# 64 first products of a dense expert mixer made ahead of its loop, in buffers shared with later tiles, instead of 40

## The chip, the core and the metric

The kernel runs on one core of a Trainium2 chip. The metric is the device time of one execution in microseconds; lower is better. The core has five engines with a queue each: TensorE (PE) multiplies matrices, VectorE (DVE) and ScalarE (ACT) work on rows, GpSimd (POOL) issues the indirect DMAs here, and SyncE (SP) issues most other DMAs. Matrix products land in PSUM, everything else lies in SBUF.

## The reference, cut to what matters

The model block has a token mixer (latent attention and an RWKV-7 scan) and then an expert mixer over 512 tokens, 1024 wide. The change concerns the second alone:

```python
def peer_ffn(h, w_query, sub_keys1, sub_keys2, expert_down, expert_up):
    q = (h @ w_query).reshape(B, S, PEER_HEADS, 2, HALF_KEY)
    ...  # top 16 of 128 keys for each half, then top 16 of the sums: expert_idx, gates
    u = jnp.take(expert_down, idx_blk, axis=0)
    act = jax.nn.gelu(jnp.einsum('bpd,bphkd->bphk', h_blk, u))
    vv = jnp.take(expert_up, idx_blk, axis=0)
    return jnp.einsum('bphk,bphkd->bpd', g_blk * act, vv)
```

Each token uses 128 of the 16384 experts (8 heads x 16).

## The kernel before, in words

**Two ways for the experts.** The tokens stand in four blocks of 128. Blocks 0 and 1 gather their experts: for each of 128 slots POOL issues an indirect DMA (line 1152) of one row per token, down and up side by side (1 MB in all), VectorE multiplies and sums (line 1156), ScalarE applies gelu and the gate, and VectorE adds the scaled row to the accumulator (line 1163). Blocks 2 and 3 (`DENSE`, `nd` = 256 tokens) instead go through all 16384 experts, as 128 groups i of 128: a first product (experts of the group x tokens, over 1024 channels, 8 steps) gives the activations, gelu follows, the gates multiply, which are zero for experts that a token hasn't chosen, and a second product adds the result times the up rows to four PSUM banks.

**The first product** is made by `dense_z(i)` (line 1202). For i < AZ + PZ = 40 it is made ahead, in plain fp32: 8 steps of one fp32 product, each of which the trace records as two matmuls, with the raw tile `u_raw` and the tokens' rows `hf`. For i from 40 on it is made in the loop: `hi_lo` (line 1186) splits `u_raw` into `uh` (a cast on ScalarE) and `ul` (a subtraction on VectorE), and the tokens' rows are split once in `dense_h` into two tiles `hh` and `hl`; three products `uh hh`, `uh hl`, `ul hh` per step make 24 matmuls. The activations of the first AF_ = 24 lie in the tile `Af`, the next 8 in a tile `A`, the last PZ = 8 go to DRAM (`zd`) and come back into `Af` in the loop.

**The stages.** (1) After the scan, `tails` computes the last blocks' query products, the top keys and the chosen indices; at each of its steps two products ahead are put in at a lower priority (ZLATE), up to ZFIRST = 24. (2) `dense_spread` (line 1241) makes the dense gates from indices and weights: for each token VectorE builds one-hot rows, TensorE multiplies them into a bank `ps_G`, and from there VectorE multiplies the first AF_ groups straight into `Af` (line 1290), while ScalarE copies the others to a buffer `g_` that is stored to the DRAM table `gd` (line 1291) once for every TB = 16 tokens. At each such step one product ahead is made. (3) The loop of `dense` (line 1294 on) runs over i: it loads `v_raw`, splits it, multiplies activations by the gates `G` (line 1334) where these were not met in PSUM, splits the result into `ch` and `cl`, and lets TensorE add the twelve 512-column matmuls of the group before. G comes from `gd` for 8 groups at a time (line 1307). The buffers of `g_` and `G` are one ring of NG = 3.

**The order of the work.** A scheduler orders each engine's instructions by priority and by its own model of their times; on the chip the order of an engine is fixed. The gathers are put in with a lower priority (LATE), two slots for each iteration of the loop, and fill what is left; they have four buffers `gl`, and POOL's next gather waits until VectorE has used one up. The order of SP's DMAs is fixed too: a load that waits for its buffer holds up those behind it. `u_raw` and `v_raw` have four buffers each.

Of the kernel before, what the change touches and what calls it, by code (L numbers as in the profile page):

```python
# [19 lines left out]
P = 128  # L20
# [13 lines left out]
PRE = 2  # L34
LATE = 1000
ZLATE = 100
ZFIRST = 24
AZ = 32
AF_ = 24
PZ = 8  # L40
NG = 3
BG = [[0.91, 2, 2, 1.0, 2.2, 2.85, 2.45, 1.0], [1.6, 2.28, 1, 0.58, 0.25, 0.5, 0.13, 0.36]]
ZSTEP = 2
ADA = 1
# [112 lines left out]
def _build(ctx, tc, nc, A, out):  # L157
# [1015 lines left out]

    TB = 16
    HB = 8
    SUB = 8
    GSC = 2.0 ** 14
    nd = len(DENSE) * P  # L1180
    dn, ahead = {}, {}
    zd = dp.tile([P, PZ, nd], F32, name="zd")
    NJ = P // SUB - AF_ // SUB
    gd = dp.tile([P, NJ, nd // TB, SUB * TB], F32, name="gd")

# [3 lines left out]

    def dense_open():  # L1190
        dn["z"] = dz = pool("dz")
        dn["h"] = [dz.tile([P, KT, nd], F32R, name=f"h{c}") for c in "hl"]
        dn["act"] = {}
        dn["first"] = dz.tile([P, AF_, nd], F32, name="Af")
        dn["hf"] = dz.tile([P, KT, nd], F32, name="hf")

    def dense_h(b, h2T):
        q = DENSE.index(b)
        S.copy(dn["hf"][:, :, q * P:(q + 1) * P], h2T)
        hi_lo(*(t[:, :, q * P:(q + 1) * P] for t in dn["h"]), h2T)  # L1200

    def dense_z(i):

        dz = dn["z"]
        hh_, hl_ = dn["h"]
        if i < AF_:
            act = dn["first"][:, i]
        elif i < AZ:
            if i % SUB == 0:
                dn["A"] = dz.tile([P, SUB, nd], F32, name="A", tag="A", bufs=(AZ - AF_) // SUB)  # L1210
            act = dn["A"][:, i % SUB]
        elif i < AZ + PZ:
            act = dz.tile([P, nd], F32, name="zp", tag="zp", bufs=2)
        else:
            act = dn["v"].tile([P, nd], F32, name="act", tag="act", bufs=2)
        u = dz.tile([P, D], F32, name="u_raw", tag="u", bufs=4)
        nc.sync.dma_start(u, A["dense"][i, 0])
        if i < AZ + PZ:
            zs = ((u, dn["hf"]),)
        else:  # L1220
            uh = dz.tile([P, D], F32R, name="uh", tag="uh", bufs=2)
            ul = dz.tile([P, D], F32R, name="ul", tag="ul", bufs=2)
            hi_lo(uh, ul, u)
            zs = ((uh, hh_), (uh, hl_), (ul, hh_))
        ps = bank("ps_z", "pr", 3)
        for k in range(KT):
            ks = slice(k * P, (k + 1) * P)
            for m, (l, h) in enumerate(zs):
                mm(ps[:, :nd], l[:, ks], h[:, k], k + m == 0, k == KT - 1 and m == len(zs) - 1)
        S.activation(act, ps[:, :nd], AF.Gelu_apprx_tanh)  # L1230
        if AZ <= i < AZ + PZ:
            nc.scalar.dma_start(zd[:, i - AZ], act)
        else:
            dn["act"][i] = act

    def dense_ahead():
        for i in range(AZ + PZ):
            dense_z(i)
            yield

# [53 lines left out]
    def dense(sel):  # L1294

        n = nd
        for _ in dense_spread(sel):
            step(ahead["z"])
        drain(ahead["z"])
        dn["v"] = de = pool("de", side="right")  # L1300
        parts = {}

        def gates_of(j):

            if j < P // SUB:
                parts[j] = dn["g"].tile([P, n // TB, SUB, TB], F32, name="G", tag="G", bufs=NG)
                nc.sync.dma_start(parts[j].rearrange("p s c t -> p s (c t)"), gd[:, j - AF_ // SUB])

        for j in range(NG - 1):
            gates_of(AF_ // SUB + j)  # L1310
        acc = [[bank(f"acc{q}{d}", *(("px", 2) if q == 0 else (("pm", 1), ("po", 1))[d])) for d in range(2)]
               for q in range(len(DENSE))]
        prev = None
        for i in range(P + 1):
            if i < P:
                if i % SUB == 0:
                    if i >= AF_:
                        gates_of(i // SUB + NG - 1)
                    if AZ <= i + SUB < AZ + PZ:
                        t = dn["first"][:, i + SUB - AZ:i + 2 * SUB - AZ]  # L1320
                        nc.sync.dma_start(t, zd[:, i + SUB - AZ:i + 2 * SUB - AZ])
                        for j in range(SUB):
                            dn["act"][i + SUB + j] = t[:, j]
                if i >= AZ + PZ:
                    dense_z(i)
                act = dn["act"].pop(i)
                v = dn["w"].tile([P, D], F32, name="v_raw", tag="v", bufs=4)
                nc.sync.dma_start(v, A["dense"][i, 1])
                vh = de.tile([P, D], F32R, name="vh", tag="vh", bufs=2)
                vl = de.tile([P, D], F32R, name="vl", tag="vl", bufs=2)  # L1330
                hi_lo(vh, vl, v)
                a3 = act.rearrange("p (s t) -> p s t", t=TB)
                if i >= AF_:
                    V.scalar_tensor_tensor(a3, a3, 1.0 / GSC, parts[i // SUB][:, :, i % SUB], op0=ALU.mult, op1=ALU.mult)
                ch = de.tile([P, n], F32R, name="ch", tag="ch", bufs=2)
                cl = de.tile([P, n], F32R, name="cl", tag="cl", bufs=2)
                hi_lo(ch, cl, act)
                cur = (ch, cl, vh, vl)
            if prev is not None:
                ch, cl, vh, vl = prev  # L1340
                for q in range(len(DENSE)):
                    qs = slice(q * P, (q + 1) * P)
                    for d in range(2):
                        ds = slice(d * 512, (d + 1) * 512)
                        for m, (a, b) in enumerate(((ch, vh), (ch, vl), (cl, vh))):
                            mm(acc[q][d], a[:, qs], b[:, ds], i == 1 and m == 0, i == P and m == 2)
            prev = cur
            yield
        gt2 = dn["z"].tile([P, D], F32, name="gt2", tag="u", bufs=4)
        nc.sync.dma_start(gt2, mrow[3:4, :].to_broadcast([P, D]))  # L1350
        for q, b in enumerate(DENSE):
            x2 = dn["w"].tile([P, D], F32, name="x2e", tag="v", bufs=4)
            y = dn["w"].tile([P, D], F32, name="y", tag="v", bufs=4)
            nc.sync.dma_start(x2, x2d[b * P:(b + 1) * P, :])
            for d in range(2):
                ds = slice(d * 512, (d + 1) * 512)
                V.tensor_tensor(y[:, ds], acc[q][d], gt2[:, ds], op=ALU.mult)
                V.tensor_tensor(y[:, ds], y[:, ds], x2[:, ds], op=ALU.add)
            nc.sync.dma_start(out[b * P:(b + 1) * P, :], y)
        yield  # L1360
# [79 lines left out]
    def drain(gen):  # L1440
        for _ in gen:
            pass
# [28 lines left out]
    drain(streams[0])  # L1471
    nz = 0
    for _ in streams[1]:
        if "z" in ahead and nz < ZFIRST:
            tc.cur_priority += ZLATE
            step(ahead["z"], ZSTEP)
            tc.cur_priority -= ZLATE
# [28 lines left out]
```

## Time and profile before

| what | us |
|---|---|
| three runs, median (lowest to highest) | 1910.42 (1905.02 to 1913.4) |
| the profiled execution | 1907.93 |
| its span, first to last instruction | 1906.2 |
| TensorE busy | 1720.0 (90%) |
| VectorE busy | 1587.9 (83%) |
| ScalarE busy | 699.8 (37%) |
| GpSimd busy | 437.2 (23%) |

Busy time is counted from the start of an instruction to its end, where instructions that overlap count once. Matmuls are pipelined, so a busy TensorE is not TensorE at its peak. The stages matter more than the shares of the whole: the token mixer takes the first half and is not touched, and the products ahead, the spread and the loop stand in the second. Times in the rows are from the start of the span.

### The profile page before, as it was taken

The numbers are of one execution on the slowest core, as the hardware profiler recorded it, in microseconds if no ns is written. First come the engines' busy times: TensorE is split into PE (matmuls) and PEld (weight loads), VectorE is DVE, ScalarE is ACT, GpSimd is POOL, SyncE is SP. The second block draws the span as 40 slices with busy tenths as digits, with TensorE's granted clock in tenths as the row PEclk, the third lists the DMA queues.
The fourth block names the chain that finished last, engine by engine and source line by source line (L and its number), as shares of the span: only waits on it lengthen the run. The fifth ranks groups of instructions, "written<-read, shape, count | busy, mean of one in ns | idle before, by whom it ended". The sixth has DMA issues, their size and how long they took to land.

```text
span 1906.2 us, 30258 instructions
## 1 busy us (share of the span) xinstructions
PE 1720.0 (90%) x11018; PEld 1472.0 (77%) x11018; DVE 1587.9 (83%) x3654; ACT 699.8 (37%) x1727; POOL 437.2 (23%) x394
## 2 busy tenths in 40 slices
PE   5879999999899999999699979779999999999992
PEld 4667877778787698988388868657899988889892
DVE  4864446559778798888689999979999999999998
ACT  1233233321323232331131133335555555555551
POOL 1210010000222210222222222022333333333333
PEclk9889999999999999999899989879999999999996
DMA  9545654166986875889899889989999999999997
GB/s 385 196 154 172 230 174 161 44 217 204 365 333 211 345 247 190 298 312 362 330 351 351 317 302 316 293 330 399 400 403 416 415 416 415 414 408 415 411 373 281
DMA packets 146274, 588.75 MB, mean 309 GB/s; under 512 B 13886, under 2 KB 41918, under 8 KB 111564
## 3 DMA queue, kind: packets, MB, share of 16 engines
q1 hardware_dynamic: 76544, 284.69, 40.4%
q0 software_dynamic: 39360, 280.51, 38.2%
q10 hardware_dynamic: 30220, 21.60, 3.6%
q8 instruction: 87, 1.43, 0.3%
q14 instruction: 63, 0.52, 0.1%
HBM read 566.81 MB, written 19.94 MB: 308 GB/s over the span
## 4 chain that ended last, share of the span: by engine, by line
issue 31%; PE 31%; DVE 13%; POOL 12%; DMA 11%; ACT 1%; POOLq 0%; SPq 0%; ACTq 0%; DVEq 0%
POOL gl L1152 12%; DMA gl<-in_experts,ii 5%; PE ps_b L237 4%; PE ps_gt L237 4%; DMA w_b<-in_w_b 3%; PE ps_q L237 3%; DVE acc L1163 3%; PE ps_z L237 2%; DVE gl L1156 2%; PE ps_ap L237 2%; PE ps_y L237 1%; PE ps_m L237 1%; PE ps_G L237 1%; PE ps_M L237 1%; PE ps_s L237 1%
## 5 line engine op out<-in xcount | busy, mean ns | idle before, releaser
L1152 POOL DMA_INDIRECT gl<-in_experts,ii x256 | 382.9, 1496 | 989.1 <-DVE acc L1163 697.0
L1156 DVE SCALAR_TENSOR_TENSOR gl<-gl,h2p 128x1024 f32<-128x1024 f32 x256 | 311.3, 1216 | 49.8 <-DMA gl<-in_experts,ii 49.5
L1163 DVE SCALAR_TENSOR_TENSOR acc<-gl,z,acc 128x1024 f32<-128x1024 f32 x256 | 326.6, 1276 | 12.6 <-ACT z L1158 7.1
L237 PE MATMUL acc<-vl,ch 128*128 128x512 f32 x512 | 204.9, 400 | 7.4 <-DVE vl L1188 7.2
L237 PE MATMUL acc<-vh,cl 128*128 128x512 f32 x512 | 204.5, 399 | 5.0 <-DVE cl L1188 4.9
L237 PE MATMUL ps_z<-hh,uh 128*128 128x256 f32 x704 | 199.4, 283 | 0.0
L237 PE MATMUL ps_z<-hh,ul 128*128 128x256 f32 x704 | 199.4, 283 | 0.0
L237 PE MATMUL acc<-vh,ch 128*128 128x512 f32 x512 | 196.9, 397 | 2.7 <-ACT ch L1187 2.7
L237 PE MATMUL ps_z<-hl,uh 128*128 128x256 f32 x704 | 199.2, 283 | 0.0
L1157 ACT ACTIVATE z<-z 128x1 f32<-128x1 f32 x256 | 51.8, 203 | 368.0 <-DVE gl L1156 367.2
L237 PE MATMUL ps_z<-hf,u_raw 128*128 128x256 f32 x640 | 156.0, 388 | 8.4 <-ACT i1T L1264 8.4
L1188 DVE TENSOR_TENSOR vl<-v_raw,vh 128x1024 fp32r<-128x1024 f32 x128 | 156.0, 1219 | 4.6 <-ACT vh L1187 4.4
L237 PE MATMUL ps_gt<-hT,w_b 128*128 128x128 f32 x1024 | 136.9, 288 | 14.5 <-DMA w_b<-in_w_b 14.4
L237 PEld LDWEIGHTS ps_gt<-hT,w_b 128*128 128x128 f32 x1024 | 127.6, 201 | 20.9 <-DMA w_b<-in_w_b 11.5
L237 PEld LDWEIGHTS ps_z<-hl,uh 128*128 128x128 f32 x704 | 135.1, 192 | 3.8
L1187 ACT CAST vh<-v_raw 128x1024 fp32r<-128x1024 f32 x128 | 134.1, 1047 | 9.6 <-PE acc L237 4.8
L237 PEld LDWEIGHTS ps_z<-hh,uh 128*128 128x128 f32 x704 | 134.7, 191 | 3.4
L237 PEld LDWEIGHTS ps_z<-hh,ul 128*128 128x128 f32 x704 | 134.8, 191 | 0.3 <-DVE ul L1188 0.2
L237 PEld LDWEIGHTS ps_z<-hf,u_raw 128*128 128x128 f32 x640 | 117.1, 194 | 21.8 <-ACT i1T L1264 8.6
L237 PE MATMUL ps_b<-hT,w_b 128*128 128x128 f32 x896 | 123.6, 288 | 7.7 <-DMA w_b<-in_w_b 6.4
L237 PE MATMUL ps_q<-h2T,w_q 128*128 128x128 f32 x1024 | 125.6, 277 | 2.1 <-DMA w_q<-in_w_query 1.4
L237 PEld LDWEIGHTS ps_b<-hT,w_b 128*128 128x128 f32 x896 | 113.3, 200 | 18.0 <-DMA w_b<-in_w_b 6.3
(445 smaller groups left out, 3299.3 us busy)
## 6 DMA issues: line engine op xcount, KB each, us to landing
u_raw<-in_dense SPq DMA_DIRECT2D x128, 512.0 KB, 7.4
v_raw<-in_dense SPq DMA_DIRECT2D x128, 512.0 KB, 8.7
w_b<-in_w_b SPq DMA_DIRECT2D x82, 512.0 KB, 4.8
w_ada<-in_w_ada SPq DMA_DIRECT2D x48, 512.0 KB, 5.4
w_q<-in_w_query SPq DMA_DIRECT2D x48, 512.0 KB, 3.7
G<-gd SPq DMA_DIRECT2D x13, 1024.0 KB, 10.6
w_o<-in_w_o SPq DMA_DIRECT2D x24, 512.0 KB, 5.1
w_out<-in_w_out SPq DMA_DIRECT2D x24, 512.0 KB, 7.0
```

The costliest lines, as they stand in the source:

```text
L237: PE.matmul(o, l, r, start=start, stop=stop)
L1152: G.indirect_dma_start(out=gl, out_offset=None, in_=A["experts"], in_offset=bass.IndirectOffsetOnAxis(ap=ii[:, s:s + 1], axis=0))
L1156: V.scalar_tensor_tensor(gl[:, :D], gl[:, :D], 1.0, h2, op0=ALU.mult, op1=ALU.mult, accum_out=z[:, 0:1])
L1157: S.activation(z[:, 1:2], z[:, 0:1], AF.Gelu_apprx_tanh)
L1163: V.scalar_tensor_tensor(acc, gl[:, D:], z[:, 1:2], acc, op0=ALU.mult, op1=ALU.add)
L1187: S.copy(hi, x)
L1188: V.tensor_tensor(lo, x, hi.bitcast(F32), op=ALU.subtract)
```

## The change

AF_ rises from 24 to 32: the first 32 groups meet their gates in PSUM, and all 32 are put into the query stage, two at each step. 32 more (PZ), the groups 32 to 63, are made ahead, where it was 16: three at each of the spread's steps, of which there are now 8 since TB is 32, and the last 8 in the loop's first eight iterations, one each. Their activations lie in the buffers that later hold the split rows of the tokens (`hh`, `hl`, eight groups each) and the split weights (`uh`, `ul`, two buffers of four groups each). The split of the tokens' rows moves from `dense_h` into the loop's iteration 52 (`dense_split`), where those buffers are free again. So the loop makes split products for the groups 64 to 127 only. The tile `A` and the trip through `zd` are gone; the table `gd` has 12 instead of 13 parts of 8 groups, its rows are stored as 1024 instead of 512 bytes, and the ring of `g_` and `G` has two buffers instead of three.

```diff
--- before.py
+++ after.py
@@ -34,11 +34,9 @@
 PRE = 2
 LATE = 1000
 ZLATE = 100
-ZFIRST = 24
-AZ = 32
-AF_ = 24
-PZ = 8
-NG = 3
+AF_ = 32
+PZ = 32
+NG = 2
 BG = [[0.91, 2, 2, 1.0, 2.2, 2.85, 2.45, 1.0], [1.6, 2.28, 1, 0.58, 0.25, 0.5, 0.13, 0.36]]
 ZSTEP = 2
 ADA = 1
@@ -1173,13 +1171,12 @@
 
 
 
-    TB = 16
+    TB = 32
     HB = 8
     SUB = 8
     GSC = 2.0 ** 14
     nd = len(DENSE) * P
     dn, ahead = {}, {}
-    zd = dp.tile([P, PZ, nd], F32, name="zd")
     NJ = P // SUB - AF_ // SUB
     gd = dp.tile([P, NJ, nd // TB, SUB * TB], F32, name="gd")
 
@@ -1189,7 +1186,6 @@
 
     def dense_open():
         dn["z"] = dz = pool("dz")
-        dn["h"] = [dz.tile([P, KT, nd], F32R, name=f"h{c}") for c in "hl"]
         dn["act"] = {}
         dn["first"] = dz.tile([P, AF_, nd], F32, name="Af")
         dn["hf"] = dz.tile([P, KT, nd], F32, name="hf")
@@ -1197,30 +1193,34 @@
     def dense_h(b, h2T):
         q = DENSE.index(b)
         S.copy(dn["hf"][:, :, q * P:(q + 1) * P], h2T)
-        hi_lo(*(t[:, :, q * P:(q + 1) * P] for t in dn["h"]), h2T)
+
+    def dense_split():
+
+        dn["h"] = [dn["z"].tile([P, KT, nd], F32R, name=f"h{c}", tag=f"h{c}", bufs=1) for c in "hl"]
+        for k in range(0, KT, 2):
+            hi_lo(*(t[:, k:k + 2] for t in dn["h"]), dn["hf"][:, k:k + 2])
 
     def dense_z(i):
 
         dz = dn["z"]
-        hh_, hl_ = dn["h"]
         if i < AF_:
             act = dn["first"][:, i]
-        elif i < AZ:
-            if i % SUB == 0:
-                dn["A"] = dz.tile([P, SUB, nd], F32, name="A", tag="A", bufs=(AZ - AF_) // SUB)
-            act = dn["A"][:, i % SUB]
-        elif i < AZ + PZ:
-            act = dz.tile([P, nd], F32, name="zp", tag="zp", bufs=2)
+        elif i < AF_ + PZ:
+            tag, n, bufs = (("hh", 8, 1), ("hl", 8, 1), ("uh", 4, 2), ("ul", 4, 2))[(i - AF_) // 8]
+            if i % n == 0:
+                dn["zp"] = dz.tile([P, n, nd], F32, name="zp", tag=tag, bufs=bufs)
+            act = dn["zp"][:, i % n]
         else:
             act = dn["v"].tile([P, nd], F32, name="act", tag="act", bufs=2)
         u = dz.tile([P, D], F32, name="u_raw", tag="u", bufs=4)
         nc.sync.dma_start(u, A["dense"][i, 0])
-        if i < AZ + PZ:
+        if i < AF_ + PZ:
             zs = ((u, dn["hf"]),)
         else:
             uh = dz.tile([P, D], F32R, name="uh", tag="uh", bufs=2)
             ul = dz.tile([P, D], F32R, name="ul", tag="ul", bufs=2)
             hi_lo(uh, ul, u)
+            hh_, hl_ = dn["h"]
             zs = ((uh, hh_), (uh, hl_), (ul, hh_))
         ps = bank("ps_z", "pr", 3)
         for k in range(KT):
@@ -1228,13 +1228,10 @@
             for m, (l, h) in enumerate(zs):
                 mm(ps[:, :nd], l[:, ks], h[:, k], k + m == 0, k == KT - 1 and m == len(zs) - 1)
         S.activation(act, ps[:, :nd], AF.Gelu_apprx_tanh)
-        if AZ <= i < AZ + PZ:
-            nc.scalar.dma_start(zd[:, i - AZ], act)
-        else:
-            dn["act"][i] = act
+        dn["act"][i] = act
 
     def dense_ahead():
-        for i in range(AZ + PZ):
+        for i in range(AF_ + PZ):
             dense_z(i)
             yield
 
@@ -1295,8 +1292,7 @@
 
         n = nd
         for _ in dense_spread(sel):
-            step(ahead["z"])
-        drain(ahead["z"])
+            step(ahead["z"], 3)
         dn["v"] = de = pool("de", side="right")
         parts = {}
 
@@ -1316,13 +1312,12 @@
                 if i % SUB == 0:
                     if i >= AF_:
                         gates_of(i // SUB + NG - 1)
-                    if AZ <= i + SUB < AZ + PZ:
-                        t = dn["first"][:, i + SUB - AZ:i + 2 * SUB - AZ]
-                        nc.sync.dma_start(t, zd[:, i + SUB - AZ:i + 2 * SUB - AZ])
-                        for j in range(SUB):
-                            dn["act"][i + SUB + j] = t[:, j]
-                if i >= AZ + PZ:
+                if i >= AF_ + PZ:
                     dense_z(i)
+                else:
+                    step(ahead["z"])
+                if i == AF_ + PZ // 2 + 4:
+                    dense_split()
                 act = dn["act"].pop(i)
                 v = dn["w"].tile([P, D], F32, name="v_raw", tag="v", bufs=4)
                 nc.sync.dma_start(v, A["dense"][i, 1])
@@ -1471,7 +1466,7 @@
     drain(streams[0])
     nz = 0
     for _ in streams[1]:
-        if "z" in ahead and nz < ZFIRST:
+        if "z" in ahead and nz < AF_:
             tc.cur_priority += ZLATE
             step(ahead["z"], ZSTEP)
             tc.cur_priority -= ZLATE
```

## Rows read from the trace of the kernel before

**Rows 1.** Busy us of PE, PEld, DVE, ACT, POOL by stage; then PEclk, DMA share, GB/s

```profile
954.00:1126.00 172.00, 153.56 (x966) 139.58 (x966) 163.13 (x596) 41.06 (x121) 42.49 (x35) 0.97 0.90 333
1126.00:1248.00 122.00, 104.71 (x841) 88.84 (x840) 118.06 (x232) 45.60 (x106) 25.71 (x9) 0.91 0.93 300
1248.00:1390.00 142.00, 132.60 (x556) 104.66 (x557) 128.42 (x179) 72.81 (x139) 38.98 (x24) 0.94 0.99 387
1390.00:1868.00 478.00, 474.81 (x3010) 427.63 (x3009) 471.32 (x622) 262.35 (x524) 160.94 (x97) 1.00 1.01 406
1868.00:1906.20 38.20, 3.28 (x12) 2.10 (x12) 30.58 (x40) 4.88 (x19) 11.55 (x7) 0.60 0.76 282
```

**Rows 2.** The gathers' last instruction (line 1163) by stage: busy us, count, clock, DMA share, GB/s

```profile
954.00:1126.00 172.00, 42.03 (x34) 0.97 0.90 333
1126.00:1248.00 122.00, 12.74 (x10) 0.91 0.93 300
1248.00:1390.00 142.00, 28.10 (x22) 0.94 0.99 387
1390.00:1868.00 478.00, 122.41 (x96) 1.00 1.01 406
1868.00:1906.20 38.20, 12.81 (x10) 0.60 0.76 282
```

**Rows 3.** Costliest groups by shape from 1000 us on: busy us, mean ns, idle before

```profile
L1163 DVE SCALAR_TENSOR_TENSOR acc<-gl,z,acc 128x1024 f32<-128x1024 f32 x162 | 206.6, 1275 | 8.1 <-POOL acc L1147 5.0 <-ACT z L1158 3.0
L1156 DVE SCALAR_TENSOR_TENSOR gl<-gl,h2p 128x1024 f32<-128x1024 f32 x160 | 194.4, 1215 | 10.3 <-DMA gl<-in_experts,ii 10.1
L1188 DVE TENSOR_TENSOR ul<-u_raw,uh 128x1024 fp32r<-128x1024 f32 x88 | 107.6, 1223 | 0.2 <-ACT uh L1187 0.2
L1334 DVE SCALAR_TENSOR_TENSOR act<-act,G 128x256 f32<-128x256 f32 x88 | 36.5, 415 | 0.0
```

**Rows 4.** TensorE in order of time about the end of the query products

```profile
1094.77 16.57 PE L237 MATMUL ps_z<-hf,u_raw 128*128 128x256 f32 x76
...
1124.74 4.49 PE L237 MATMUL ps_z<-hf,u_raw 128*128 128x256 f32 x12 [8.39 <-ACT i1T L1264]
```

**Rows 5.** TensorE in order of time, in one iteration of the late loop

```profile
1385.28 0.28 PE L237 MATMUL ps_z<-hh,ul 128*128 128x256 f32 x1
1385.40 0.39 PE L237 MATMUL acc<-vh,ch 128*128 128x512 f32 x1
...
1388.15 0.28 PE L237 MATMUL ps_z<-hh,uh 128*128 128x256 f32 x1
```

**Rows 6.** Groups of VectorE instructions in the spread, 1126 to 1248 us

```profile
L1290 DVE SCALAR_TENSOR_TENSOR Af<-Af,ps_G 128x96 f32<-128x96 f32 x64 | 14.3, 246 | 2.9 <-ACT g__9404 L1288 1.7 <-ACT g__9700 L1288 0.4 <-ACT g__9774 L1288 0.4
L1188 DVE TENSOR_TENSOR ul<-u_raw,uh 128x1024 fp32r<-128x1024 f32 x5 | 6.1, 1216 | 0.2 <-ACT uh L1187 0.2
```

**Rows 7.** TensorE's group of gate products in the spread, 1126 to 1248 us

```profile
L237 PE MATMUL ps_G<-og,o 128*128 128x128 f16 x512 | 44.1, 232 | 15.3 <-DVE og L1279 15.3
```

**Rows 8.** Columns as in rows 1, two stretches at the spread's end

```profile
1220.00:1240.00 20.00, 10.10 (x95) 8.02 (x92) 18.55 (x39) 6.90 (x14) 0.00 (x0) 0.68 0.79 248
1240.00:1260.00 20.00, 13.98 (x57) 10.15 (x57) 14.93 (x24) 8.52 (x21) 5.31 (x4) 0.56 0.89 305
```

**Rows 9.** VectorE in order of time at the loop's start

```profile
1260.36 1.28 DVE L1163 SCALAR_TENSOR_TENSOR acc<-gl,z,acc 128x1024 f32<-128x1024 f32 x1 [4.96 <-POOL acc L1147]
...
1266.37 0.43 DVE L1334 SCALAR_TENSOR_TENSOR A<-A,G 128x256 f32<-128x256 f32 x1 [3.25 <-DMA G<-gd]
```

**Rows 10.** Waits of the SP queue, 1100 to 1400 us: total, times, longest

```profile
SPq L1307 <- DMA gd<-g__9848: 10.8, 1, 10.8
```

**Rows 11.** DMA from 960 us on: totals, then issues with size and us to landing

```profile
DMA packets 94241, 351.92 MB, mean 372 GB/s; under 512 B 7744, under 2 KB 35392, under 8 KB 70848
...
G<-gd SPq DMA_DIRECT2D x13, 1024.0 KB, 10.6
...
gd<-g__9626 ACTq DMA_DIRECT2D x1, 832.0 KB, 7.4
```

## The prediction

> **What bounds the kernel now.** I first cut the last 950 us into five stages and read the busy time of each engine [rows 1]: the end of the token mixer's tail with the query products (954 to 1126), the spreading of the gates (1126 to 1248), the loop's iterations without a first product (1248 to 1390), those with one (1390 to 1868), and the rest (1868 to 1906). Nothing before 954 is touched. The reader should see that three resources are nearly full. VectorE is busy 911.5 of 952.2 us, so idle 40.7. TensorE is busy 474.8 of 478 in the long stage. The DMA engines are at 1.01 there, at 406 GB/s. Second, I counted the gathered experts per stage by their last VectorE instruction [rows 2]: 34, 10, 22, 96 and 10. They run in every stage, behind the dense work, and ten are left when the dense products have ended. So a shorter dense loop alone moves gathers into the last stage; the end comes earlier only if VectorE's total work falls, or its idle time. Therefore I make the sum on VectorE and test it against TensorE and the DMA.
>
> **The change on VectorE.** Products 40 to 63 are now made ahead in plain fp32, so 24 subtractions `ul` go, 1.223 us each [rows 3]: 29.4 us off. Products 24 to 31 meet their gates in PSUM, so 8 multiplications in the loop go, 0.415 us each: 3.3 us off. For that the 64 PSUM gate instructions grow from 96 to 128 columns a partition. One took 246 ns with 96 [rows 6], the loop's one 415 with 256 [rows 3], so 1.06 ns a column and 34 ns for 32: 64 x 0.034 = 2.2 us on. The split of the tokens' rows moves from the query stage to iteration 52, two times 1024 columns either way (1.22 us each by the `ul` row): nothing net. Sum: 30.5 us less. All of this VectorE work lies in stages where it is 90 to 99% busy and gathers wait for it.
>
> **The change on TensorE.** Ahead, 76 fp32 matmuls took 16.57 us [rows 4], so 16 of a product take 3.49, and 24 products 83.8. In the loop a split product is 24 matmuls at 0.12 us [rows 5], 2.88; 24 of them are 69.1. So TensorE gets 14.7 us more, out of the loop and into the front. To 1868 it has 48.3 us idle (18.4 + 17.3 + 9.4 + 3.2) [rows 1].
>
> **Where the 24 go, and what they cost there.**
> Eight more come before the spread, since the first PSUM gate reads all 32. They need 27.9 us of TensorE, which idles 8.4 there today [rows 4], so the first gate comes 19.5 us later. VectorE then has gathers alone. A product's 512 KB in 3.49 us are 150 GB/s, which leaves 256 of 406; a gathered row tile (1 MB) takes 4.1 us at that, of which VectorE works 2.49 (1.275 + 1.215 [rows 3]). So it idles 39% of 19.5: 7.6 us on. The bounds are 0 (the 24th product had come well before the gate today, or other work fills it) and 19.5 (the fixed order puts no gather there).
> Eight more are made in the spread (24 instead of 16), between the one-hot products. TensorE then needs 83.8 + 44.1 [rows 7] = 127.9 us. VectorE's 118.1 [rows 1] loses the five `ul` that run there today (6.1 [rows 6]) and gains 2.2: 114. So the stage is TensorE's now, and grows by about 6 us. VectorE's idle time, 3.9 today, could grow to 14, or not at all if four more gathers go in: 0 to 10, I take 5.
> The last eight stand in the loop's first eight iterations, 2.75 us each for the other product's twelve matmuls [rows 5], so 6.2 with one. Gathers fill VectorE there.
>
> **The start of the loop.** TensorE worked in short bursts at the end of the spread, and its granted clock was 0.68 and 0.56 [rows 8], mostly the lower of its two levels (1.2 and 2.4 GHz). VectorE idled 5.0 us for POOL's clearing of the accumulator and 3.25 for the gates G [rows 9], whose load had waited 10.8 us on SP for the last store of the spread [rows 10], with the `v_raw` loads queued behind it. The gates are now first needed at iteration 32 instead of 24, and eight longer iterations lie ahead of it. I take the 3.3 us off; the 5.0 belong to the change of gathered blocks, which stays: bounds 0 to 8.2 off.
>
> **Edits that I cost at nothing.** NG falls from 3 to 2. A G load can leave when the group before is used up and has eight iterations, 22 us, to land, against 10.6 today [rows 11]. In the spread a buffer is written again one step (now two of today's 7.6 us, so 15) after its store was issued. The store landed after 7.4 us with 832 KB [rows 11] and is now 1536 KB: between 7.4 and, by size, 13.7, and I take the upper, as it is nearest to G's 1 MB in 10.6. Beyond 15 every second step would pay the difference, since ScalarE's copy out of PSUM waits, with the gelu of the products ahead queued behind it. SP issues the same loads, 24 of them earlier; in eight iterations a `u_raw` load that waits for its buffer stands ahead of the `v_raw` loads, covered by the four `v_raw` buffers (four iterations of 6.2 us). ScalarE loses 24 casts and eight DMA issues, and was busy 262 of 478 us. POOL's queue holds the gathers alone, which wait for VectorE as before. The rings that hold products are free long before their old use: the first `ul` buffer after iteration 59, its next user is 64.
>
> **Sum.** 1906.2 - 30.5 + 7.6 + 5 - 3.3 = 1885.0 us of span. The profiled execution took 1.7 us more than its span, and the median of the runs lies 2.5 above it: 1889.2, so 1889. With the bounds of the unknown costs, 1872 (nothing on, 8.2 off) to 1909 (29.5 on, nothing off), and mostly 1880 to 1900. The test on TensorE: for the loop to end some 15 us earlier than now, it has to win back about 30 us, of 48.3 idle and of the low clock, which gave 0.62 of full speed for 40 us [rows 8] and so cost up to 15.
>
> **Rivals.**
> *The front is covered entirely.* More matmuls between the bursts keep the clock at its upper level, VectorE finds gathers throughout, and the loop starts without its waits: 30.5 + 8.2 off, 1867.5 of span, 1872. For it: the low clock stands exactly where TensorE has only bursts [rows 8]. Against: in the query stage both engines are near full already. The Trainium skill, TensorE: Matmul & The Clock Gate, section HAM oscillation, says that pauses between batches of matmuls put the clock back to half. By that rule the added products would save the cold stretch, and the trace agrees, with 0.56 behind the bursts.
> *The DMA is the bound.* The bytes are nearly the same: 2.1 MB less for the trip of eight products through DRAM and 2.1 for the smaller gate table, of 351.9 from 960 on [rows 11]. At 406 GB/s that is 10.3 us, with the same idle time in the front, where the share is 0.90 and 0.93: 1895.9, so 1900. For it: 1.01 in the long stage. Against: the front has 26 us of DMA time free, and the 24 moved loads are 31 at 406 GB/s. The Trainium skill, DMA: Bandwidth & Descriptors, section Where 436 GB/s comes from, holds some 358 GB/s for the limit of one core's reads from HBM. By that rule the DMA would bind all the stages and this rival would be the likeliest; the trace disagrees, with 406 over 478 us.
> *TensorE is the bound and recovers nothing.* Its order is fixed, the idle times in the front are waits for VectorE and ScalarE that stay, and the extra 14.7 us end the loop later, with ten gathers left as now: 1920.9, so 1925, slower. It decides against the change if TensorE recovers less than 14.7 of its 48.3 us, or, read on VectorE, if its idle time grows by over 30.5. For it: fp32 products cost TensorE more than split ones, and they move into stages where it is busy 153.6 of 172 and 104.7 of 122. Against: 8.4 us of its idle time is a single wait [rows 4], and 17.3 lie in the spread itself, between bursts that products can fill [rows 1].
>
> **Chances.** Forecast 0.52, covered front 0.12, DMA 0.20 (1894 to 1906), TensorE 0.16 (1912 to 1932). A measurement of this kernel can tell about 0.5%, 9.6 us, from no change. Faster: 0.50 + 0.12 + 0.10 = 0.72; within: 0.02 + 0.10 + 0.04 = 0.16; slower: 0.12. The range runs from 1868, in the covered front's case, to 1916, the lower part of TensorE's, and leaves out about 0.15.
>
> **What would show it.** Right: the 32nd product comes 15 to 25 us after today's 24th; the spread ends near 1270; the loop's end near 1850; ten to twelve gathers left there; VectorE idle about 50 us after 954. Wrong: VectorE waiting for Af's products or for ScalarE's copies in the spread, long gaps without gathers there, more than 15 gathers left at the end, or `ch` waiting for G in the loop.

## The result and the profile after

| | before | after |
|---|---|---|
| median of six runs, us | 1910.89 | 1889.5 |
| lowest to highest | 1898.86 to 1913.4 | 1886.86 to 1896.19 |
| the profiled execution | 1907.93 | 1893.01 |
| its span | 1906.2 | 1891.2 |
| VectorE busy from 954 us on | 911.5 | 883.0 |
| VectorE idle from 954 us on | 40.7 | 54.3 |
| TensorE busy from 954 us on | 869.0 | 874.7 |

The ratio after to before is 0.9901, 95% interval 0.9879 to 0.9924: about 1% faster. The forecast was 1889.

**Stages.** The table of stages of the kernel after answers to [rows 1] (busy us and count of PE, PEld, DVE, ACT, POOL; PEclk; DMA share; GB/s). The borders are those of its own stages: query products with the products ahead, spread, iterations whose first product was made ahead, iterations with a split first product, rest.

```profile
954.00:1152.00 198.00, 182.47 (x1085) 164.21 (x1084) 179.25 (x619) 43.87 (x138) 48.57 (x40) 0.96 0.92 342
1152.00:1274.00 122.00, 120.81 (x915) 102.51 (x914) 121.69 (x233) 43.56 (x117) 18.59 (x15) 1.00 0.93 334
1274.00:1494.00 220.00, 206.04 (x871) 164.60 (x870) 197.77 (x278) 109.52 (x220) 60.82 (x38) 0.98 0.99 386
1494.00:1858.00 364.00, 362.09 (x2304) 327.27 (x2302) 359.64 (x475) 199.84 (x399) 134.03 (x73) 1.00 1.01 406
1858.00:1891.20 33.20, 3.32 (x13) 2.10 (x12) 24.60 (x32) 3.52 (x14) 7.32 (x4) 0.64 0.65 243
sum 937.20, PE 874.73 PEld 760.69 DVE 882.95 ACT 400.30 POOL 269.34; mean PE 174.95 PEld 152.14 DVE 176.59 ACT 80.06 POOL 53.87
```

The front is 26 us longer (198 against 172), the spread as long as before (122), but now with both engines busy all through it. The two parts of the loop and the rest, 658.2 us before (142 + 478 + 38.2), take 617.2. In the late loop nothing has changed in kind: TensorE is busy 362.1 of 364 us, VectorE 359.6, the DMA at 1.01.

**Gathers.** Their last instruction by stage (VectorE busy us and count, clock, DMA share, GB/s) answers to [rows 2].

```profile
954.00:1152.00 198.00, 50.23 (x40) 0.96 0.92 342
1152.00:1274.00 122.00, 16.56 (x13) 1.00 0.93 334
1274.00:1494.00 220.00, 47.27 (x37) 0.98 0.99 386
1494.00:1858.00 364.00, 93.18 (x74) 1.00 1.01 406
1858.00:1891.20 33.20, 10.15 (x8) 0.64 0.65 243
```

Eight are left at the end where ten were.

**VectorE's groups** from 954 us on (busy us, mean ns, idle before, its cause) answer to [rows 3], which begin at 1000 us, and to the gate instruction of [rows 6].

```profile
L1161 DVE SCALAR_TENSOR_TENSOR acc<-gl,z,acc 128x1024 f32<-128x1024 f32 x171 | 218.1, 1276 | 5.5 <-ACT z L1156 5.1
L1154 DVE SCALAR_TENSOR_TENSOR gl<-gl,h2p 128x1024 f32<-128x1024 f32 x170 | 206.6, 1215 | 28.9 <-DMA gl<-in_experts,ii 28.4
...
L1185 DVE TENSOR_TENSOR ul<-u_raw,uh 128x1024 fp32r<-128x1024 f32 x64 | 78.2, 1222 | 0.0
...
L1329 DVE SCALAR_TENSOR_TENSOR act<-act,G 128x256 f32<-128x256 f32 x64 | 26.6, 416 | 0.0
...
L1287 DVE SCALAR_TENSOR_TENSOR Af<-Af,ps_G 128x128 f32<-128x128 f32 x64 | 15.8, 277 | 0.2
```

The subtractions `ul` fell from 88 to 64 at the same 1.22 us each, and the gate instruction in the spread takes 277 ns instead of 246. VectorE's wait for gathers' rows in front of their first instruction (L1154) is 28.4 us. The row of the kernel before for the same stretch, from 954 us on (total, times, longest), has 15.4:

```profile
DVE gl L1156 <- DMA gl<-in_experts,ii: 15.4, 19, 2.6
```

**Where VectorE's new idle time stands.** VectorE in order of time at the loop's start (start, us, instruction, idle time before it and its cause; the `zp` are gate multiplications of the products ahead) answers to [rows 9].

```profile
1280.14 1.22 DVE L1154 SCALAR_TENSOR_TENSOR gl<-gl,h2p 128x1024 f32<-128x1024 f32 x1 [4.45 <-DMA gl<-in_experts,ii]
...
1297.28 2.77 DVE L1329 SCALAR_TENSOR_TENSOR zp<-zp,G 128x256 f32<-128x256 f32 x8 [9.34 <-DMA G<-gd]
...
1320.65 2.10 DVE L1329 SCALAR_TENSOR_TENSOR zp<-zp,G 128x256 f32<-128x256 f32 x6 [3.80 <-DMA G<-gd]
```

Before, this place held one wait of 3.25 us for G; now there are two, 13.1 us together. VectorE's order is fixed, so the splits and gathers behind the `zp` wait too. The way of that G shows on the queues: the last store of the spread (ScalarE's queue), SP's wait for it, which answers to [rows 10], and the load (SP's queue).

```profile
1271.66 0.52 ACTq L1288 DMA_DIRECT2D gd<-g__9924  x1
```

```profile
SPq L1303 <- DMA gd<-g__9924: 10.9, 1, 10.9
```

```profile
1288.94 0.33 SPq L1303 DMA_DIRECT2D G<-gd  x1
```

From the store's issue to the load's 17.3 us passed, and 8.3 more until VectorE went on: 25.6. Before, the same two steps began at 1246.9 and 1261.5 and ended at 1266.4: 19.5. The one store whose landing is recorded answers to [rows 11]:

```profile
gd<-g__9294 ACTq DMA_DIRECT2D x1, 1536.0 KB, 19.8
```

**The clock at the spread's end**, where [rows 8] had 0.68 and 0.56 (columns as in the first table):

```profile
1240.00:1260.00 20.00, 20.00 (x162) 17.01 (x161) 19.95 (x41) 6.74 (x19) 0.94 (x1) 1.00 0.85 288
1260.00:1274.00 14.00, 14.00 (x100) 11.87 (x99) 14.00 (x26) 5.81 (x14) 4.35 (x3) 1.00 0.89 288
```

TensorE has no bursts there any more, and the granted clock stays at its upper level.

### The profile page after: what moved, and what is told of

Its sections match the earlier page's. It is cut to its first block, busy times and chain, and to the rows that moved or that the text cites. A ratio compares the mean times of both kernels' runs of the same rounds, so it can differ in the third digit from the quotient of the medians.

```text
span 1891.2 us, 29771 instructions
## 1 busy us (share of the span) xinstructions
PE 1730.1 (91%) x10826; PEld 1470.5 (78%) x10826; DVE 1560.6 (83%) x3624; ACT 674.2 (36%) x1705; POOL 428.7 (23%) x394
## 4 chain that ended last, share of the span: by engine, by line
PE 30%; issue 30%; DVE 13%; DMA 13%; POOL 13%; ACT 1%; POOLq 0%; SPq 0%; ACTq 0%; DVEq 0%
POOL gl L1150 12%; DMA gl<-in_experts,ii 8%; PE ps_b L235 4%; PE ps_gt L235 3%; PE ps_q L235 3%; PE ps_ap L235 2%; DVE acc L1161 2%; DVE gl L1154 2%; DMA w_ada<-in_w_ada 2%; DMA w_b<-in_w_b 2%; PE ps_y L235 2%; PE ps_z L235 2%; PE ps_M L235 1%; PE ps_m L235 1%; PE ps_s L235 1%
## 5 line engine op out<-in xcount | busy, mean ns | idle before, releaser
L1150 POOL DMA_INDIRECT gl<-in_experts,ii x256 | 373.6, 1460 | 984.0 <-DVE acc L1161 701.3
L1154 DVE SCALAR_TENSOR_TENSOR gl<-gl,h2p 128x1024 f32<-128x1024 f32 x256 | 311.4, 1217 | 64.0 <-DMA gl<-in_experts,ii 63.0
L235 PE MATMUL ps_z<-hf,u_raw 128*128 128x256 f32 x1024 | 246.6, 388 | 4.2 <-DMA u_raw<-in_dense 4.2
L235 PEld LDWEIGHTS ps_z<-hf,u_raw 128*128 128x128 f32 x1024 | 189.7, 194 | 27.2 <-issue 4.7
L235 PE MATMUL ps_z<-hh,ul 128*128 128x256 f32 x512 | 144.9, 283 | 0.0
L235 PE MATMUL ps_z<-hh,uh 128*128 128x256 f32 x512 | 144.8, 283 | 0.0
L235 PE MATMUL ps_z<-hl,uh 128*128 128x256 f32 x512 | 144.8, 283 | 0.0
L235 PE MATMUL ps_gt<-hT,w_b 128*128 128x128 f32 x1024 | 132.2, 282 | 10.5 <-DMA w_b<-in_w_b 10.4
L235 PEld LDWEIGHTS ps_q<-h2T,w_q 128*128 128x128 f32 x1024 | 121.5, 192 | 3.8 <-ACT h2T L1022 1.3
L235 PEld LDWEIGHTS acc<-vl,ch 128*128 128x128 f32 x512 | 96.9, 189 | 33.4 <-DVE vl L1185 15.5
L235 PEld LDWEIGHTS acc<-vh,cl 128*128 128x128 f32 x512 | 97.0, 190 | 29.3 <-DVE cl L1185 9.6
```

The source lines that it names most:

```text
L235: PE.matmul(o, l, r, start=start, stop=stop)
L1150: G.indirect_dma_start(out=gl, out_offset=None, in_=A["experts"], in_offset=bass.IndirectOffsetOnAxis(ap=ii[:, s:s + 1], axis=0))
L1154: V.scalar_tensor_tensor(gl[:, :D], gl[:, :D], 1.0, h2, op0=ALU.mult, op1=ALU.mult, accum_out=z[:, 0:1])
```

## The experiments

The theory is the prediction's: the end follows VectorE, its work plus its idle time. The rivals are the DMA and TensorE as the bound of the late loop, and, on the new idle time, that a wait taken away at the loop's start comes back elsewhere. Ratios are to the kernel before. All edits but one are made on the kernel after.

**hold_gates: the gates of the products ahead stand later in VectorE's order.**

```diff
-                hi_lo(vh, vl, v)
+                vls.append(hi_lo(vh, vl, v))
...
-                    V.scalar_tensor_tensor(a3, a3, 1.0 / GSC, ...)
+                    with tc.issue_after(vls[i - 2].ins) if i < AF_ + PZ else nullcontext():
+                        V.scalar_tensor_tensor(a3, a3, 1.0 / GSC, ...)
```

> The changed kernel, with the gate multiplications of groups 32 to 63 put behind the vl of two iterations before on VectorE, so that none of them stands in the queue ahead of its iteration. In the changed kernel they stand at the loop's start and VectorE waits 13.1 us there for the table G. If VectorE's work and idle time set the end, most of the 13.1 us are won: 1877 to 1881 us against 1889.5. If the DMA or TensorE sets it, the wait only moves: 1886 to 1893.

Measured: 0.9894 (0.9863 to 0.9926), the same as the change itself. The list of VectorE's waits from 954 us on (total, times, longest) no longer has G; in its place stands, where the kernel after had 28.4:

```profile
DVE gl L1154 <- DMA gl<-in_experts,ii: 43.0, 32, 5.2
```

The wait did not go, it changed its name: 13.1 us for G became 14.6 more for gathers' rows. From 1300 to 1340 us the DMA is at its limit in this kernel:

```profile
1300.00:1340.00 40.00, 31.61 (x128) 25.14 (x126) 30.17 (x37) 13.06 (x34) 14.37 (x9) 0.91 1.02 417
```

So the late G is not worth 13 us: what VectorE would do instead needs rows, and with the DMA at 1.02 these came no sooner.

**hold_spaced: the same, and the eight products in the loop one every third iteration,** so that their loads don't fall together.

```diff
-                else:
+                elif i % 3 == 0:
                     step(ahead["z"])
```

> The changed kernel with the gate multiplications held behind their iteration, as in the first of these runs, and the loop's eight products ahead made in every third iteration up to 21 instead of in the first eight: the eight loads of 512 KB and the tables G no longer meet at the loop's start. There the wait for G had only turned into waits for gathers (43.0 us in all against 28.4), with the DMA at 1.01 to 1.02. If the DMA's burst at the loop's start is what keeps VectorE waiting: its idle time from 954 us on falls from 54 to under 45 us, 8 to 12 us less, ratio 0.984 to 0.986. If these waits are set by the four gather buffers: 0.989 to 0.991.

Measured: 0.9932 (0.9907 to 0.9957); nothing gained. The waits for gathers are 31.8 us here and G has none, but 8.1 us more of waits for `vh` stand at another place (10.5 against 2.4), and VectorE's idle time is 51.6. The burst was not what held the loop's start back, or what it freed was taken again at once. That the four gather buffers set these waits stays possible; no run changes their number.

**vl_twice: VectorE made to work more.** The subtraction `vl` is done twice for the groups 40 to 63.

```diff
                 hi_lo(vh, vl, v)
+                if 40 <= i < 64:
+                    V.tensor_tensor(vl, v, vh.bitcast(F32), op=ALU.subtract)
```

> The changed kernel, with the subtraction vl made a second time in iterations 40 to 63 (the same values again): 24 more VectorE instructions of 1.22 us, as many as the change took away, and nothing else for TensorE or the DMA. If VectorE sets the end: 27 to 29 us more, 1917 to 1919. If the DMA or TensorE sets it and VectorE has slack: under 8 us more, below 1898.

Measured: 1.0041 (1.0018 to 1.0065), so 1.4 points, some 27 us, above the changed kernel, for 29 us of added work. The two last stages show how it reaches the end:

```profile
1494.00:1858.00 364.00, 362.50 (x2298) 328.22 (x2297) 360.92 (x473) 201.54 (x397) 137.43 (x70) 1.00 1.00 401
1858.00:1916.50 58.50, 9.49 (x51) 7.38 (x49) 48.02 (x62) 9.27 (x34) 22.16 (x13) 0.63 0.79 298
```

VectorE is as full as before in the late loop, and 17 gathers instead of 8 are left behind it. So 24 subtractions put back cost what the 24 removed `ul` should have given.

**v_reuse: the DMA relieved.** The odd groups from 65 to 111 don't load `v_raw` but take the tile of the group before (their own up rows are left out): 12.6 MB less.

```diff
-                v = dn["w"].tile([P, D], F32, name="v_raw", tag="v", bufs=4)
-                nc.sync.dma_start(v, A["dense"][i, 1])
+                if not (64 <= i < 112 and i % 2):
+                    v = dn["w"].tile([P, D], F32, name="v_raw", tag="v", bufs=4)
+                    nc.sync.dma_start(v, A["dense"][i, 1])
```

> The changed kernel without 24 of the v_raw loads (odd groups 65 to 111 take the tile of the group before, so that part of the up rows is left out): 12.6 MB less in the loop's late part, no instruction less on an engine. If the DMA sets the end: 12.6 MB at 406 GB/s, 31 us less, 1858. If VectorE sets it: 0 to 5 us less, 1885 to 1890, and the DMA share of the late loop falls from 1.01 to about 0.93.

Measured: 0.9900 (0.9862 to 0.9938), nothing. The late loop runs at the same pace with the DMA below its limit:

```profile
1494.00:1858.00 364.00, 360.43 (x2283) 325.04 (x2282) 358.17 (x476) 198.56 (x399) 147.94 (x74) 1.00 0.96 370
```

**z_two_terms: TensorE relieved.** The same groups leave out the term `uh hl` of the split product, 8 of 24 matmuls.

```diff
             zs = ((uh, hh_), (uh, hl_), (ul, hh_))
+            if i < 112 and i % 2:
+                zs = ((uh, hh_), (ul, hh_))
```

> The changed kernel without the product of uh with the tokens' low part in the odd groups 65 to 111 (that term is left out): 192 matmuls of 0.12 us, 23 us less on TensorE, the other engines as before. If TensorE sets the end: 1866 to 1868. If VectorE sets it: 0 to 5 us less, 1885 to 1890, with TensorE idle in the late loop.

Measured: 0.9927 (0.9897 to 0.9956), nothing gained. TensorE was not idle in the late loop, as expected, but full up to its last product (343.6 of 346.4 us), which came at 1840 instead of 1862 us. VectorE had its work still to do, 28 us of it in the rest:

```profile
1494.00:1858.00 364.00, 343.81 (x2128) 307.15 (x2126) 356.80 (x471) 201.07 (x393) 154.40 (x70) 0.98 1.00 400
1858.00:1900.00 42.00, 0.00 (x0) 0.00 (x0) 28.46 (x35) 5.47 (x22) 13.07 (x8) 0.51 0.71 263
```

**vl_less: VectorE relieved.** The same groups leave out the subtraction `vl` and use that of the group before, 29 us less of VectorE's work.

```diff
-                vl = de.tile([P, D], F32R, name="vl", tag="vl", bufs=2)
-                hi_lo(vh, vl, v)
+                if not (64 <= i < 112 and i % 2):
+                    vl = de.tile([P, D], F32R, name="vl", tag="vl", bufs=2)
+                if 64 <= i < 112 and i % 2:
+                    S.copy(vh, v)
+                    vl = prev[3]
+                else:
+                    hi_lo(vh, vl, v)
```

> The changed kernel without the subtraction vl in the odd groups 65 to 111, which take the low part of the group before (so that part of the up rows' low term is wrong): 24 VectorE instructions of 1.22 us less, every matmul and every DMA as before. If VectorE's work still sets the end in the changed kernel: 25 to 29 us less, ratio to the kernel before 0.975 to 0.977. If another resource stands right behind it (TensorE busy 362 of 364 us in the late loop, the DMA at 1.01): under 10 us less, ratio above 0.985.

Measured: 0.9955 (0.9923 to 0.9987), nothing gained and rather slower than the changed kernel; the traced execution lies 9.5 us below this kernel's median. This is the miss that matters: VectorE's work fell by 29.3 us (853.6 from 954 us on), and its idle time rose by 28.6 (to 82.9). The late loop and its largest wait (from 1494 us on; 6.8 us in the kernel after):

```profile
1494.00:1858.00 364.00, 342.37 (x2097) 301.01 (x2096) 331.42 (x443) 188.81 (x390) 104.14 (x76) 0.99 1.01 410
```

```profile
DVE gl L1154 <- DMA gl<-in_experts,ii: 32.4, 28, 4.0
```

In VectorE's order the freed time was filled with gathers: 79 in this stage instead of 74, and none left behind the loop. Their rows did not come in time, at a DMA share of 1.01. VectorE waited, TensorE waited for `ch` and `cl` (11.0 and 10.4 us from 1274 us on, where the kernel after has 0.6 and 5.2), and the last product came at 1883 instead of 1862 us:

```profile
L235 PE MATMUL acc<-vh,cl x512: 387/389/797, 1272.5 to 1883.3; 128*128 128x512 f32 x171
```

"VectorE's work alone" falls here. Two readings of the late rows stay open: that the DMA could bring them no sooner, or that VectorE's new order, with more gathers ahead of the dense work, asked for them too early. A gather took no longer to land than in the kernel after (9.8 us in the median of this stage, against 10.1), and behind 1858 us the held-up dense products kept TensorE busy for 25.7 of 32.5 us, with the DMA at 0.26.

**all_three: the last three edits at once.** If the late loop is long because three resources are full together, only relief of all of them shows.

```diff
+            if i < 112 and i % 2:
+                zs = ((uh, hh_), (ul, hh_))
...
-                v = dn["w"].tile([P, D], F32, name="v_raw", tag="v", bufs=4)
-                nc.sync.dma_start(v, A["dense"][i, 1])
+                if not (64 <= i < 112 and i % 2):
+                    v = dn["w"].tile([P, D], F32, name="v_raw", tag="v", bufs=4)
+                    nc.sync.dma_start(v, A["dense"][i, 1])
...
-                vl = de.tile([P, D], F32R, name="vl", tag="vl", bufs=2)
-                hi_lo(vh, vl, v)
+                if 64 <= i < 112 and i % 2:
+                    S.copy(vh, v)
+                    vl = prev[3]
+                else:
+                    vl = de.tile([P, D], F32R, name="vl", tag="vl", bufs=2)
+                    hi_lo(vh, vl, v)
```

> This kernel does at once, in the 24 odd groups from 65 to 111, what v_reuse, z_two_terms and vl_less did one at a time: no load of v (the tile of the group before is used again), no second of the three gate terms, no vl subtraction (the vl of the group before is used again). It leaves out those parts of the dense products. Taken from the late loop: 24 x 512 KB = 12.6 MB, some 31 us at the 406 GB/s of that stage; 23 us of TensorE; 24 x 1.22 = 29 us of VectorE. If the late loop is long because these three are full at the same time, so that each one alone gave nothing, the three together give what the smallest of them frees: 23 to 29 us less than the changed kernel, ratio to the kernel before 0.975 to 0.979. If something that none of the three edits touches sets it (the order written out for VectorE, the gathers' buffers, GpSimd), the ratio stays above 0.985 as in the three runs before. Between the two, part of each.

Measured: 0.9812 (0.9772 to 0.9851), 0.89 points or 17 us below the changed kernel, from edits of which each alone gave nothing. The late loop and the rest:

```profile
1494.00:1858.00 364.00, 347.29 (x2131) 307.23 (x2129) 350.77 (x474) 204.05 (x411) 112.83 (x77) 1.00 0.98 389
1858.00:1872.00 14.00, 0.00 (x0) 0.00 (x0) 8.76 (x10) 0.99 (x4) 0.00 (x0) 0.50 0.50 188
```

VectorE's work is 25.5 us below that of the kernel after (857.4), nearly as in vl_less, but its idle time is 60.6 and not 82.9. From 1494 us on it waits for gathers' rows less than half as long as in vl_less, with about as many gathers in the late loop (78 against 79):

```profile
DVE gl L1154 <- DMA gl<-in_experts,ii: 12.8, 15, 2.0
```

That speaks for the DMA, and not VectorE's order, as what made the rows late in vl_less. The 17 us are part of the 23 to 29 expected. TensorE is busy 347 of the 357 us up to its last product, VectorE 351 of 364; the DMA is at 0.98 in the mean and still at 1.00 from 1600 to 1800 us. Whether TensorE's relief was needed for it, or the DMA's and VectorE's would have done, was not tried.

**ahead_56 and psum_24: 56 products ahead instead of 64,** the first with 32 groups in PSUM and 24 in the rings, the second with 24 and 32.

```diff
-PZ = 32
+PZ = 24
...
-                if i == AF_ + PZ // 2 + 4:
+                if i == 52:
```

> The changed kernel with 56 products ahead instead of 64: none in the loop's first eight iterations, and groups 56 to 63 made split in the loop. VectorE gets 8 subtractions more, 9.8 us, and the loop's start loses eight loads of 512 KB (4.2 MB, 10 us of DMA time). If a product ahead is worth its subtraction: 0.5% slower than the changed kernel, ratio to the kernel before about 0.995. If the eight loads at the loop's start cost as much as they save there, where the DMA is full and gathers are waited for: no difference, ratio 0.990, and VectorE's waits for gathers fall by some 10 us.

```diff
-AF_ = 32
+AF_ = 24
```

> The changed kernel with 24 groups meeting their gates in PSUM and 32 in the rings, so 56 ahead: as many as in the run with 56, but eight of them in the loop's first eight iterations and only 24 in front of the spread. The first gate should come some 20 to 28 us earlier than in the changed kernel. If the later first gate costs idle time of VectorE (9.9 us more in the front than before the change), that time comes back and pays for the eight subtractions and eight multiplications more (13.1, less 2.2): ratio 0.989 to 0.992. If gathers had filled the front and only VectorE's work counts: 10.9 us more, ratio 0.996.

Measured: 0.9934 (0.9900 to 0.9968) and 0.9972 (0.9943 to 1.0001). VectorE's work is 893.0 and 892.3 us, 10.0 and 9.3 more than with 64 (eight `ul` are 9.8), its idle time 45.7 and 49.9. So the eight products more are worth their subtractions less some of the new idle time. psum_24 came out as if VectorE's work alone counted. In it the spread's first gate product came at 1126.9 us, about where it did before the change (1129.1):

```profile
L235 PE MATMUL ps_G<-og,o x512: 217/218/233, 1126.9 to 1241.9; 128*128 128x128 f16 x171
```

Which of the two has the better place for its eight products can't be told from intervals that overlap.

**before_psum_32: the PSUM part alone,** on the kernel before: 32 groups meet their gates in PSUM, still 40 products ahead.

```diff
-ZFIRST = 24
+ZFIRST = 32
...
-AF_ = 24
+AF_ = 32
```

> The kernel before with one part of the change alone: 32 groups meet their gates in PSUM, all of them in front of the spread, still 40 products ahead, eight of them through DRAM. VectorE: 8 multiplications less (3.3 us), PSUM gates longer (2.2), so 1.1 less; TensorE the same work. The first gate comes 19 to 28 us later. If the delay is idle time for VectorE: 7 to 10 us slower, ratio 1.004 to 1.005. If gathers cover it: ratio 0.999 to 1.001.

Measured: 1.0068 (1.0038 to 1.0099), slower by some 13 us. The first gate product (the first start in this row; 1129.1 us before) came 25 us later:

```profile
L237 PE MATMUL ps_G<-og,o x512: 218/222/314, 1154.4 to 1268.5; 128*128 128x128 f16 x171
```

VectorE's work rose by 3.1 us (1.1 less was expected) and its idle time by 6.3. This half of the change costs by itself. Part of it stands in the spread, which has eight products ahead left instead of 16: from 1154 to 1270 us the granted clock is 0.76 and VectorE is idle for 11.4 of 116 us, where it was 3.9 of 122. The whole change fills that place with 24 products, so the gain comes from the 24 split products that are no longer made, and the two halves are not independent.

**tb_16: steps of the spread as before.** TB 16 and NG 3, one or two products at each of 16 steps.

```diff
-NG = 2
+NG = 3
...
-    TB = 32
+    TB = 16
...
-        for _ in dense_spread(sel):
-            step(ahead["z"], 3)
+        for t, _ in enumerate(dense_spread(sel)):
+            step(ahead["z"], 1 + t % 2)
```

> The changed kernel with 16 tokens in a step of the spread (one and two products ahead in turn, so 24 again) and three buffers for g_ and G, as before the change: only the size of the stores and the number of buffers go back. A store is 768 KB instead of 1536 and should land in 7 to 10 us instead of 17 to 20, so G's first table comes some 9 us earlier; the stores have 512-byte pieces again. If the step's size matters through the wait for G: up to 9 us less, ratio 0.986. If that wait only trades places with others: ratio 0.989 to 0.992.

Measured: 0.9919 (0.9891 to 0.9947), no difference from the change. The stores are 768 KB again, and G landed 21.8 us after the last store's issue, against 25.6. The wait for it stayed:

```profile
DVE zp L1329 <- DMA G<-gd: 12.3, 2, 8.5
```

**spread_four: the last eight products in the spread too,** four at each step, none in the loop.

```diff
-            step(ahead["z"], 3)
+            step(ahead["z"], 4)
```

> The changed kernel with four products ahead in each of the spread's eight steps instead of three, so that all 64 are made when the loop starts. TensorE is busy 120.8 of 122 us in the spread already; eight products more are 28 us there, and 28 less at the loop's start. If the spread takes them as VectorE fills up with gathers: no difference, ratio 0.988 to 0.992. If VectorE waits for TensorE there: its idle time grows by 10 us or more, ratio above 0.994.

Measured: 0.9915 (0.9891 to 0.9940), no difference. The spread's last gate came at 1290 instead of 1272 us, the wait for G fell to 1.4 us, and VectorE's idle time is 51.7 us. Where these eight stand made no difference that these runs can tell.

## Why the prediction was right, step by step

**The sum as a whole.** Time, sign and range hold. On the span the sum was 21.2 us; the profiled execution shows 15.0, the medians 21.4 (this execution lies 3.5 us above its median). In that execution VectorE's work fell by 28.6 us and its idle time rose by 13.6: 9.9 in the front, 3.6 less in the spread, 8.7 more in the loop up to the first split product, 1.3 less behind it. The forecast had 7.6, 5 and 3.3 less for the first three. So the work and the sign of the idle time were foreseen; that the median came within half a microsecond of 1889 is luck, since single terms missed by up to 12 us in both directions.

**VectorE's work: right.** 30.5 us off were forecast, 28.6 measured. All its prices hold: `ul` at 1.222 us, the gate instruction 31 ns longer (34 forecast). vl_twice shows that a microsecond of VectorE's work put in costs about one at the end.

**The front: right in kind, too small.** The first gate product came 22.8 us later (19.5 forecast). VectorE's idle time to the spread rose from 8.9 to 18.75, by 9.9 us (7.6 forecast), and it was the wait foreseen: 15.2 us for gathers' rows, where 8.3 were, and 3.3 for ScalarE's `z` of the gathers. TensorE's wait of 8.4 us went, but it now waits 4.2 for a load of `u_raw` and 3.2 for the transposes of the indices.

**The spread: wrong in size.** It was to grow by 6 us and VectorE to idle 5 more. It stayed at 122, and VectorE's idle time fell from 3.9 to 0.3, with 13 gathers instead of 10. TensorE did become its bound (120.8 of 122 us), but the matmuls became cheaper: those of the gate products took 40.2 us instead of 44.1, and the granted clock was 1.00 instead of 0.91 in the mean. This is the step of the covered front's rival, that products between the bursts keep the clock up. The page that it cites (the Trainium skill, TensorE: Matmul & The Clock Gate, section HAM oscillation) says that pauses between batches put the clock back to half; this trace agrees, with 1.00 in place of 0.68 and 0.56. The prediction's sum of the two busy times was also too long: 25 products at its 3.49 us leave 33.5 of the 120.8 us to the gate products, whose own row says 40.2, so the two overlap. TensorE's total rose by 5.8 us and not by 14.7; 3.9 of the difference are the gate products', the rest no row here tells apart.

**The loop's start: the step that failed.** 3.3 us were to fall away there, with the gates "now first needed at iteration 32 instead of 24". VectorE's order does not go by iterations: the multiplications of the products ahead need nothing but G, the scheduler put eight of them some 16 us behind the spread, as far as the first one stood before, and G came 6 us later than before. The landing of the store was also taken too short, 13.7 us at most with a slack of 15; the recorded one took 19.8, and ScalarE waited 4.1 us for one buffer. So G's wait grew by 9.9 us instead of falling by 3.3. The 5.0 us for POOL's clearing, which the prediction kept, did fall away: the clearing now stands at 1190 us, in the spread, and nothing waits for it. With 6.4 us of new waits for gathers' rows VectorE's idle time rose from 13.6 us (1248 to 1390) to 22.2 (1274 to 1494). hold_gates then showed that this did not decide the time: without the wait for G the same time is lost to the gathers' rows.

**The rivals.** The DMA alone is not the bound (v_reuse), nor TensorE alone (z_two_terms), and TensorE recovered the added work, as the forecast wanted. But the argument that only VectorE's work and idle time count was too simple: vl_less took as much of VectorE's work off as the change and gave nothing, since VectorE then waited for gathers' rows in the late loop, at a DMA share of 1.01. What the change did, and vl_less did not, was to relieve all three behind the spread. From the two tables of stages, for the loop and the rest together (before: 1248 to 1906 us; after: 1274 to 1891):

| | before | after | less by |
|---|---|---|---|
| length, us | 658.2 | 617.2 | 41.0 |
| TensorE busy, us | 610.7 | 571.4 | 39.3 |
| VectorE busy, us | 630.3 | 582.0 | 48.3 |
| DMA, MB (GB/s by length) | 259.8 | 240.8 | 19.0 |

At 406 GB/s the 19 MB are 47 us. So all three loads fell by about what the length fell by, for a front that is 26 us longer and took in nine more gathers (53 against 44). all_three repeats the pattern in another place and gains again. That this is why the change gained is an inference from these runs: a kernel that gives VectorE alone the change's relief, and leaves TensorE's and the DMA's work where it was, was only made in the late loop (vl_less).

**The signs given beforehand.** The spread's end (1274, near 1270) and VectorE's idle time (54.3, about 50) are as told. The loop ended at 1862 instead of near 1850, and eight gathers were left instead of ten to twelve: the two make up for each other in part. The 32nd product's gelu came 36 us after the 24th's before (1151.7 against 1115.6), not 15 to 25. Of the signs of being wrong one came in kind: the multiplications in front of `ch` waited for G.

## What to carry to other kernels

Where two engines and the DMA were all above 98% in one stage, relieving one of them gained nothing in three runs, and VectorE work added ahead of that stage cost in full (vl_twice). Look for a change that takes the same work from all of them at once and puts it where they have slack, and count it on each of the three.

A wait that stands alone in an engine's list is not yet a gain: ask whether what would run in its place has its data. And a fixed order by priority asks for an operand when its instruction could run by the scheduler's model, not at the iteration in which its result is used.

## What the runs showed of the hardware

A store of 1536 KB took 19.8 us to land in the spread, where the DMA engines' share was 0.93, against 7.4 for 832 KB [rows 11]: 2.7 times the time for 1.85 times the bytes. One store is recorded in each of these traces; hold_spaced, vl_less, all_three and ahead_56 each show one of 1536 KB too, at 19.4 to 19.9 us. The load behind such a store started 17.3 us after the store's issue, 14.3 with 768 KB (tb_16). With fp32 products between the bursts the granted clock at the spread's end was 1.00 instead of 0.68 and 0.56, and the 512 gate products took 40.2 us instead of 44.1.
